# Pair products and their sums' transfers at other places, and the end of a layer shared out anew over the engines

## The chip, the cores and the metric

The kernel runs on one core of one Trainium2 chip. A core has five engines that each work through their own queue in order: TensorE (PE, matrix products into PSUM, with the weight loads shown apart as PEld), VectorE (DVE), ScalarE (ACT), GpSimd (POOL) and SyncE (SP, which here only issues transfers). POOL issues transfers too, those that add to what already lies in SBUF. The metric is the device time of one execution in microseconds; lower is better.

## The reference, cut to what matters

Two layers, each on 256 frames of 1024 channels. A layer normalises x, projects it with one wide matrix, splits the result among three token mixers and their gates, and adds the merged result back:

```python
h = _rms(x, norm_g[l])
proj = h @ w_in[l]
(gq, gk, gv, ga, gz, bq, bk, bv, iq, ik, iw, bz,
 cq, ck, cv, cz, gate) = jnp.split(proj, SPLIT_AT, axis=-1)
y_a = _gla(gq, gk, gv, ga, ...) * jax.nn.silu(gz)
y_b = _dsa(bq, bk, bv, iq, ik, iw, ...) * jax.nn.silu(bz)
y_c = _diff(cq, ck, cv, ...) * jax.nn.silu(cz)
g = jax.nn.sigmoid(gate.reshape(B, T, N_BRANCH, D_MODEL))
merged = (g[:, :, 0] * (y_a @ w_br[l, 0]) + g[:, :, 1] * (y_b @ w_br[l, 1])
          + g[:, :, 2] * (y_c @ w_br[l, 2]))
x = x + merged @ w_out[l]
```

`_gla` is a gated linear attention over chunks of 64 frames, `_dsa` scores all keys with a small indexer (iq, ik, iw), keeps the best 64 for each query and attends over those, `_diff` is the difference of two softmax attentions. Each `gate` block is a 256 x 1024 by 1024 x 512 product.

## The kernel before, in words

**Weights in two parts.** A product at full float32 accuracy is made of three products of rounded parts. A *unit* is a piece of a weight matrix of 128 x 1024 values. `Stream.split` makes of it `whi` (L230, on ACT, a copy rounded to fp32r) and `wlo` (L236, on DVE, the difference); `mm3` then issues three matmuls for each piece of a product. There are five pairs of `whi` and `wlo` buffers (`BUFS["wt"]`) and four buffers for raw units (`BUFS["raw"]`), which SP loads (L200).

**The order of the work.** `ORDER` (L36) names the pieces of a layer; `plan()` makes of it `PLAN`, a list of 104 units per layer, and `USE`, which says which places of that list a piece uses. An ordinary piece such as `bq`, `gv` or `gate0` has four units of twelve matmuls of 512 columns; `iq` and `bz` are made transposed, and hold their four units for the whole of the piece; `p..` (branch products) and `out..` have two units each.

**Pairs.** The gate blocks 2 and 3 (pair A) and 5 and 1 (pair B) are made together with Strassen's seven products instead of eight: `A1` to `A7`, `B1` to `B7`. Each of these has two units of six matmuls. Four of the seven need sums of weight blocks (`SUMS`): product 5 uses the sum called t1, product 6 t2, product 4 t4, product 7 t3. A sum is built in an SBUF tile by transfers: SP loads a first block (`begin_sum`, L217), POOL then adds a second block with an accumulating transfer (`add`, L206). t2 is t1's tile with one more block added, and t4 is t2's with one more, so those additions are issued from `split` right after t1's, or t2's, own split, and have to land before the next product of that pair is split. t1 and t3 get their first addition in `begin_sum`. `SUMS_AHEAD, SUMS_ADD = 12, 2` (L72): the load stands in the code at the split 12 places before the sum's own, the addition two splits later. The sums' tiles come from a pool of eight (`w4`), shared with key and probability tiles.

**The mixers as tasks.** The attention work is written as generators which `Flow.pump` advances; the pump is called after each group of matmuls that belongs to one of a unit's two halves (twelve matmuls' unit: two pumps). `Y` (L96) says how many pumps a task waits at each step: `dsa0` between the end of `iq` and the start of the indexer, `att0` between a selection of keys and the attention over them.

**Who sets the order on the engines.** The program is built under a planner (`tile.TileContext(nc, schedule_with_timeline_sim=True)`) that places each instruction in its engine's queue by the order of the code and by when its own timing model expects the operands. `order(a, b)` and `hold` put one instruction behind another in a queue without a wait. On the chip each queue is then worked through in that order.

**The end of a layer** (L1121 to L1144). The output product goes in four accumulators, `(n, t)` for column half and row half; row half t = 0 is finished first for both n, then t = 1. After each one DVE adds it to x (L1138) and ACT squares and sums that half (`sumsq`, L316). After n = 1, `norm_in(l + 1, t)` adds the two sums (`norm_scale`, DVE L320), raises to the power -1/2 on POOL (L321), scales the two halves of x (`norm_half`, DVE L327), transposes them on PE (L121) and writes the two parts of h, `hTh` on ACT (L336) and `hTl` on DVE (L337). The last layer writes x out instead.

Of the kernel before, what the change touches and what calls it, by code (L numbers as in the profile page):

```python
# [8 lines left out]
F32 = mybir.dt.float32  # L9
# [23 lines left out]

PAIRS = {"A": ("gate2", "gate3"), "B": ("gate5", "gate1")}

ORDER = ["bq", "cq", "ck", "gate4", "cz", "bk", "cv", "gq", "iq", "bv", "B1", "B5", "gv", "B2", "B6", "gz", "B4", "A1",  # L36
         "B3", "bz", "B7", "A5", "gate0", "A2", "p20", "A6", "p00", "A4", "p21", "A3", "A7", "p10", "p01", "p11",
         "out00", "out10", "out01", "out11"]
NAMES = [n for c in ORDER if c[0] not in PAIRS for n in (c,)] + [n for c in PAIRS.values() for n in c]


# [27 lines left out]

plan()  # L70
NPLAN = len(PLAN)
SUMS_AHEAD, SUMS_ADD = 12, 2  # L72

POOL_LO = [USE[c][i] for c, i in []]

# [13 lines left out]
MERGE_WAIT = 0  # L93
WARM = 14
AHEAD1 = (0, 2)
Y = dict(sm0=0, qk0=1, qk=3, dsa0=8, dec0=7, diff0=0, gla0=0, att0=3, top=1, blog=12, bpT=11, by=14, clog=4, cpT=2, cy=2, za=17, q2=5, st=27, go=9, sums=0)  # L96
BUFS = dict(w2=8, kp=28, w4=8, ev=2, raw=4, wt=5, ahead=21)


# [1 line left out]
def trunk(ctx: ExitStack, tc: tile.TileContext, x0, x1, units, wsmall, pack, ptmp, wa2b, out):  # L101
# [43 lines left out]
    def w4(shape, dt=F32, n="w4"):  # L145
        return sp.tile(shape, dt, tag="w4", bufs=BUFS["w4"], name=nm(n))
# [31 lines left out]
    class Stream:  # L178
# [6 lines left out]
        def hold(self, j, evac):  # L185

            if j in self.splits:
                for a, b in zip(self.splits[j], evac):
                    tc.add_manual_dep(a.ins, b.ins.name, NOSYNC, reason="order")
            else:  # L190
                self.after[j] = evac

# [12 lines left out]
            u = l * NUNIT + (UNIT[two] + 2 if what in ("t2", "t3") else UNIT[one] + (2 if what == "t4" else 0))  # L205
            G.dma_start(self.sums[l, "t3" if what == "t3" else "t1", pair, i], units[u + i], accum_op=OP.add)  # L206

        def begin_sum(self, j):
            for j, adds in ((j, False), (j - SUMS_ADD, True)):
                if j >= L * NPLAN or PLAN[j % NPLAN][0] not in ("t1", "t3"):  # L210
                    continue
                l, (what, pair, i) = j // NPLAN, PLAN[j % NPLAN]
                if adds:
                    self.add(l, what, pair, i)
                else:
                    t = self.sums[l, what, pair, i] = w4([P, 1024], F32, "sum")
                    order(nc.sync.dma_start(t, units[l * NUNIT + UNIT[PAIRS[pair][1]] + i]), self.loaded)  # L217

        def tiles(self):
            hi = wp.tile([P, 1024], F32R, tag="whi", bufs=BUFS["wt"], name=nm("whi"))  # L220
# [3 lines left out]

        def split(self):
            j = len(self.made)
            self.begin_sum(j + SUMS_AHEAD)
            raw, (hi, lo) = self.raws[j], self.tiles()
            what, *arg = PLAN[j % NPLAN]
            a = A.activation(hi, raw, AF.Copy)  # L230
            if j % NPLAN in POOL_LO:
                self.splits[j] = (a,)
                for h in HV:
                    G.tensor_sub(lo[:, h], raw[:, h], hi[:, h].bitcast(F32))
            else:
                self.splits[j] = (a, V.tensor_sub(lo, raw, hi.bitcast(F32)))  # L236
            if what in ("t1", "t2"):
                self.add(j // NPLAN, "t2" if what == "t1" else "t4", *arg)
            if j in self.after:
                self.hold(j, self.after[j])  # L240
# [79 lines left out]
        a = V.scalar_tensor_tensor(v, ss[t][:, 0:1], EPS, ss[t][:, 1:2], op0=OP.add, op1=OP.add)  # L320
        return r, a, G.tensor_tensor(r, v, half[:, :1], op=OP.pow)  # L321

    def norm_half(t, hf, r):

        ps = [at([P, 2, P], "hps") for _ in range(2)]
        h = w2([P, 512], F32, "h")
        a = V.tensor_scalar_mul(h, xs[t][:, HV[hf]], r)  # L327
        for j in range(4):
            TE.transpose(ps[j % 2][:, j // 2], h[:, j * P:(j + 1) * P], ident)
        return ps, a  # L330
# [7 lines left out]
                                       op0=OP.mult, op1=OP.subtract))  # L338

    def norm_in(l, t):  # L340
        r, _, _ = norm_scale(t)
        ps = [norm_half(t, hf, r)[0] for hf in range(2)]
        for k in range(KD8):
            e = evac(l, t, k, ps)
        if t == 0:
            ws.hold(l * NPLAN + HOLD, e)

    def project(jobs):

# [188 lines left out]
    for l in range(L):  # L538
# [584 lines left out]
        for h, n, t in ((0, 0, 0), (0, 0, 1), (0, 1, 0), (0, 1, 1), (1, 0, 0), (1, 1, 0), (1, 0, 1), (1, 1, 1)):  # L1123
            cols = [(po[n, t], slice(0, CH))]
            if (l, n, t) == (L - 1, 1, 1):
                cols = [(po[n, t][:, :256], slice(0, 256)), (po_end, slice(256, CH))]
            for ps, c in cols:
                for k in range(4):
                    wh, wl = ws.need(use(l, f"out{n}{h}")[k // 2])
                    hi, lo = mT[h, t]  # L1130
                    mm3(ps, hi[:, k], lo[:, k], wh[:, k % 2, c], wl[:, k % 2, c],
                        h == 0 and k == 0, h == 1 and k == 3)
                    if k % 2:
                        flow.pump()
                if h == 0:
                    continue
                xc = xs[t][:, n * CH + c.start:n * CH + c.stop]
                V.tensor_add(xc, ps, xc)  # L1138
                if l + 1 == L:
                    nc.sync.dma_start(out[t * P:(t + 1) * P, n * CH + c.start:n * CH + c.stop], xc)  # L1140
                else:
                    sumsq(t, n)
                    if n == 1:
                        norm_in(l + 1, t)  # L1144


def _lay_out(inputs):
# [74 lines left out]
```

## Time and profile before

| what | value |
|---|---|
| median of 3 runs | 607.3 us (606.71 to 607.91) |
| the profiled execution | 605.64 us, of which its span, first to last instruction, 603.9 us |
| granted TensorE clock | 1.000 |
| PE busy | 586.6 us (97%) |
| PEld busy | 494.6 us (82%) |
| DVE busy | 495.6 us (82%) |
| ACT busy | 378.8 us (63%) |
| POOL busy | 96.3 us (16%) |
| transfers | 121.82 MB, 202 GB/s on the mean |

Engine times are busy time and overlap each other. A row of a timeline has the start, the duration, the engine, the source line, the operation, the tile written and those read, and in brackets how long the engine had been idle and what ended that. In the list of waits a row names who waited for whom, the total in us, how many times, and the longest. The chain is the sequence of work that ended last, each piece with its start and its length. The matmuls' ends are modelled, so idle time of PE is best read from the starts.

### The profile page before, as it was taken

To read this page: it belongs to the slowest core of one execution; us is meant where nothing else is said; L and a number is where in the kernel's file an instruction comes from. 1 tells how busy PE (TensorE), PEld (TensorE's weight loads), DVE (VectorE), ACT (ScalarE), POOL (GpSimd) and SP (SyncE) were. 2 spreads that over 40 slices of the span, in tenths; PEclk is the share of its full clock that TensorE was granted. 3 is DMA by queue.
4 is the path that set the end of the run, shared out by engine and by line. 5 is a ranking of instruction groups with operands and counts; after the bars stand their busy time and mean duration, and the time that the engine had idled before them with its cause. 6 is when DMAs were issued, how large, how long until landed. Compare 5 with 4: busy or idle time off the path is not lost.

```text
span 603.9 us, 8831 instructions
## 1 busy us (share of the span) xinstructions
PE 586.6 (97%) x3118; PEld 494.6 (82%) x3118; DVE 495.6 (82%) x813; ACT 378.8 (63%) x651; POOL 96.3 (16%) x127
## 2 busy tenths in 40 slices
PE   7999999999998999999999999999999989899997
PEld 4888888998887987788878888889888878787886
DVE  6868969888979988699587796797889899759982
ACT  5759767786747465564466765876775658646540
POOL 6034212011111052000011240300102202210000
PEclk9999999999999999999999999999999999999999
DMA  8654678347897389556545445862599962994731
GB/s 334 229 185 140 216 256 234 132 139 199 277 267 221 118 246 303 173 186 236 174 140 199 151 155 196 269 217 71 175 262 277 279 226 43 341 247 138 237 114 69
DMA packets 34027, 121.82 MB, mean 202 GB/s; under 512 B 3776, under 2 KB 4160, under 8 KB 33984
## 3 DMA queue, kind: packets, MB, share of 16 engines
q1 hardware_dynamic: 29376, 104.49, 49.0%
q0 software_dynamic: 4608, 16.78, 14.5%
q8 instruction: 24, 0.39, 0.2%
q14 instruction: 19, 0.16, 0.1%
HBM read 120.21 MB, written 1.05 MB: 201 GB/s over the span
## 4 chain that ended last, share of the span: by engine, by line
PE 61%; DMA 15%; DVE 12%; issue 6%; ACT 3%; POOL 1%; SPq 0%; ACTq 0%; POOLq 0%; DVEq 0%
DMA sum<-in_units 12%; PE p L118 7%; PE out L118 6%; DVE wlo L236 5%; PE gate L118 5%; PE iq L118 4%; PE gq L118 4%; PE cq L118 4%; PE ck L118 4%; PE cz L118 4%; PE bk L118 4%; PE cv L118 4%; PE bz L118 4%; PE bq L118 3%; DMA raw<-in_units 3%
## 5 line engine op out<-in xcount | busy, mean ns | idle before, releaser
L236 DVE TENSOR_TENSOR wlo<-raw,whi 128x1024 fp32r<-128x1024 f32 x172 | 209.6, 1229 | 38.1 <-ACT whi L230 37.1
L230 ACT ACTIVATE whi<-raw 128x1024 fp32r<-128x1024 f32 x172 | 180.5, 1061 | 90.0 <-DMA raw<-in_units 28.9
L230 ACT ACTIVATE whi<-sum 128x1024 fp32r<-128x1024 f32 x32 | 33.5, 1060 | 42.5 <-DMA sum<-in_units 30.1
L236 DVE TENSOR_TENSOR wlo<-sum,whi 128x1024 fp32r<-128x1024 f32 x32 | 38.5, 1217 | 20.2 <-ACT whi L230 20.1
L290 POOL TENSOR_SCALAR v<-ss 128x4 f32<-128x4 f32 (+1 forms) x24 | 11.4, 475 | 195.6 <-DVE ss L390 94.9
L206 POOL DMA_DIRECT2D sum<-in_units x32 | 28.3, 903 | 85.8 <-DVE wlo L236 25.5
L291 POOL TENSOR_TENSOR r<-v,half 128x4 f32<-128x4 f32 (+1 forms) x24 | 33.6, 1401 | 1.8
L118 PE MATMUL p<-wlo,yTh 128*128 128x512 f32 x64 | 25.2, 395 | 1.5 <-DVE wlo L236 1.5
L118 PE MATMUL out<-wlo,mTh 128*128 128x512 f32 (+1 forms) x72 | 26.2, 368 | 0.0
L118 PE MATMUL p<-whi,yTh 128*128 128x512 f32 x64 | 25.3, 395 | 0.9 <-DVE gate L960 0.9
L118 PE MATMUL q<-wlo,sh 128*128 128x512 f32 x64 | 25.4, 397 | 0.7 <-DVE wlo L236 0.7
L118 PE MATMUL out<-whi,mTh 128*128 128x512 f32 (+1 forms) x72 | 26.0, 366 | 0.0
L118 PE MATMUL out<-whi,mTl 128*128 128x512 f32 (+1 forms) x72 | 25.7, 368 | 0.0
L118 PE MATMUL q<-whi,sl 128*128 128x512 f32 x64 | 25.1, 392 | 0.0
L118 PE MATMUL gate<-whi,hTl 128*128 128x512 f32 x64 | 25.0, 393 | 0.0
L118 PE MATMUL q<-whi,sh 128*128 128x512 f32 x64 | 25.0, 395 | 0.0
L118 PE MATMUL gate<-wlo,hTh 128*128 128x512 f32 x64 | 24.9, 390 | 0.0
L118 PE MATMUL gate<-whi,hTh 128*128 128x512 f32 x64 | 24.7, 395 | 0.0
L118 PE MATMUL p<-whi,yTl 128*128 128x512 f32 x64 | 24.6, 390 | 0.0
L118 PE MATMUL q<-whi,hTh 128*128 128x512 f32 x48 | 19.6, 408 | 1.5 <-ACT gate L1041 1.5
L118 PE MATMUL q<-wlo,hTh 128*128 128x512 f32 x48 | 18.8, 392 | 0.0
L118 PE MATMUL q<-whi,hTl 128*128 128x512 f32 x48 | 18.7, 390 | 0.0
(351 smaller groups left out, 1751.5 us busy)
## 6 DMA issues: line engine op xcount, KB each, us to landing
raw<-in_units SPq DMA_DIRECT2D x176, 512.0 KB, 4.3
sum<-in_units POOLq DMA_DIRECT2D x32, 512.0 KB, 9.4
sum<-in_units SPq DMA_DIRECT2D x16, 512.0 KB, 6.5
wsr<-in_wsmall SPq DMA_DIRECT2D x2, 416.0 KB, 6.2
xe<-in_x SPq DMA_DIRECT2D x1, 584.0 KB, 3.6
x<-in_x SPq DMA_DIRECT2D x1, 512.0 KB, 8.0
out<-xe SPq DMA_DIRECT2D x2, 256.0 KB, 2.0
pt<-in_ptmp SPq DMA_DIRECT2D x1, 384.0 KB, 9.5
```

Source lines behind the costliest of these rows:

```text
L118: return self.put(nc.tensor.matmul(*a, **k))
L206: G.dma_start(self.sums[l, "t3" if what == "t3" else "t1", pair, i], units[u + i], accum_op=OP.add)
L230: a = A.activation(hi, raw, AF.Copy)
L236: self.splits[j] = (a, V.tensor_sub(lo, raw, hi.bitcast(F32)))
L290: G.tensor_scalar(v, ss, 1.0 / dim, EPS, op0=OP.mult, op1=OP.add)
L291: G.tensor_tensor(r, v, half[:, :n], op=OP.pow)
```

## The change

Four edits. (1) `ORDER`: B1 moves from behind bv to right behind iq; gv and bv change places; A5 moves from behind B7 to right behind A1; gate0 comes before B7; A6 comes before p20 instead of behind it. (2) `SUMS_ADD` becomes 4, so that the first addition of t1 and t3 stands four splits behind its load in the code instead of two; `begin_sums` treats t1 and t3 each with its own distance (both 12). (3) `Y`: `dsa0` 8 to 6, `att0` 3 to 6; `st` is read nowhere. (4) The end of layer 0: the sum of squares of (t, n) = (0, 1) goes from ACT to DVE (`sumsq_v`, L310); the scaling of x for t = 0 goes from DVE to ACT; the `wlo` of the next layer's second unit is put behind `norm_scale`'s DVE instruction for t = 0; and ACT's sum of squares for (1, 1) is put behind the last ACT instruction of `norm_in` for t = 0. `hold` learns to skip a missing part.

```diff
-ORDER = ["bq", "cq", "ck", "gate4", "cz", "bk", "cv", "gq", "iq", "bv", "B1", "B5", "gv", "B2", "B6", "gz", "B4", "A1",
-         "B3", "bz", "B7", "A5", "gate0", "A2", "p20", "A6", "p00", "A4", "p21", "A3", "A7", "p10", "p01", "p11",
-         "out00", "out10", "out01", "out11"]
+ORDER = ["bq", "cq", "ck", "gate4", "cz", "bk", "cv", "gq", "iq", "B1", "gv", "B5", "bv", "B2", "B6", "gz", "B4",
+         "A1", "A5", "B3", "bz", "gate0", "B7", "A2", "A6", "p20", "p00", "A4", "p21", "A3", "A7", "p10", "p01",
+         "p11", "out00", "out10", "out01", "out11"]
-SUMS_AHEAD, SUMS_ADD = 12, 2
+SUMS_AHEAD, SUMS_ADD = {"t1": 12, "t3": 12}, 4
-Y = dict(sm0=0, qk0=1, qk=3, dsa0=8, dec0=7, diff0=0, gla0=0, att0=3, top=1, blog=12, bpT=11, by=14, clog=4, cpT=2, cy=2, za=17, q2=5, st=27, go=9, sums=0)
+Y = dict(sm0=0, qk0=1, qk=3, dsa0=6, dec0=7, diff0=0, gla0=0, att0=6, top=1,
+         blog=12, bpT=11, by=14, clog=4, cpT=2, cy=2, za=17, q2=5, st=30, go=9, sums=0)
                 for a, b in zip(self.splits[j], evac):
-                    tc.add_manual_dep(a.ins, b.ins.name, NOSYNC, reason="order")
+                    if b is not None:
+                        tc.add_manual_dep(a.ins, b.ins.name, NOSYNC, reason="order")
-        def begin_sum(self, j):
-            for j, adds in ((j, False), (j - SUMS_ADD, True)):
-                if j >= L * NPLAN or PLAN[j % NPLAN][0] not in ("t1", "t3"):
-                    continue
...
+        def begin_sums(self, j):
+
+            for what, ahead in SUMS_AHEAD.items():
+                for n, adds in ((j + ahead, False), (j + ahead - SUMS_ADD, True)):
+                    if n >= L * NPLAN or PLAN[n % NPLAN][0] != what:
+                        continue
+                    l, (_, pair, i) = n // NPLAN, PLAN[n % NPLAN]
+                    if adds:
+                        self.add(l, what, pair, i)
+                    else:
+                        t = self.sums[l, what, pair, i] = w4([P, 1024], F32, "sum")
+                        order(nc.sync.dma_start(t, units[l * NUNIT + UNIT[PAIRS[pair][1]] + i]), self.loaded)
-            self.begin_sum(j + SUMS_AHEAD)
+            self.begin_sums(j)
-    def norm_half(t, hf, r):
+    def norm_half(t, hf, r, on_act=False):
...
-        a = V.tensor_scalar_mul(h, xs[t][:, HV[hf]], r)
+        x = xs[t][:, HV[hf]]
+        a = A.activation(h, x, AF.Copy, scale=r) if on_act else V.tensor_scalar_mul(h, x, r)
     def norm_in(l, t):
-        r, _, _ = norm_scale(t)
-        ps = [norm_half(t, hf, r)[0] for hf in range(2)]
+        r, v, _ = norm_scale(t)
+        if t == 0:
+            ws.hold(l * NPLAN + 1, (None, v))
+        ps = [norm_half(t, hf, r, t in (0,))[0] for hf in range(2)]
...
+        return e
...
-                    sumsq(t, n)
+                    square = (sumsq_v if (t, n) == (0, 1) else sumsq)(t, n)
+                    if (t, n) == (1, 1):
+                        order(square, behind[0])
                     if n == 1:
-                        norm_in(l + 1, t)
+                        behind = norm_in(l + 1, t)
```

More of the change, by code (lines that the diff above doesn't have):

```diff
@@ L71 @@
 NPLAN = len(PLAN)
-SUMS_AHEAD, SUMS_ADD = 12, 2
-POOL_LO = [USE[c][i] for c, i in []]
+SUMS_AHEAD, SUMS_ADD = {"t1": 12, "t3": 12}, 4
+POOL_LO = []
 def columns(*widths):
@@ L206, in add @@
             G.dma_start(self.sums[l, "t3" if what == "t3" else "t1", pair, i], units[u + i], accum_op=OP.add)
-        def begin_sum(self, j):
-            for j, adds in ((j, False), (j - SUMS_ADD, True)):
-                if j >= L * NPLAN or PLAN[j % NPLAN][0] not in ("t1", "t3"):
-                    continue
[L212 to L217, printed above, removed]
+        def begin_sums(self, j):
[9 more added lines that the diff above has]
+                        order(nc.sync.dma_start(t, units[l * NUNIT + UNIT[PAIRS[pair][1]] + i]), self.loaded)
         def tiles(self):
```

## The prediction

> **What bounds the kernel now.** I read the page first, then the list of PE's waits, then the timelines around each wait.
>
> ```profile
> PE 586.6 (97%) x3118; PEld 494.6 (82%) x3118; DVE 495.6 (82%) x813; ACT 378.8 (63%) x651; POOL 96.3 (16%) x127
> ...
> raw<-in_units SPq DMA_DIRECT2D x176, 512.0 KB, 4.3
> ```
>
> PE is busy for 97% of the span, and the change takes away no matmul, so only PE's waits can go. They are few:
>
> ```profile
> PE blog L118 <- DVE sd L896: 2.6, 2, 1.3
> PE hps L121 <- DVE h L327: 2.0, 2, 1.2
> PE pT L121 <- DVE bp L722: 1.7, 2, 1.0
> PE q L118 <- ACT gate L1041: 1.5, 2, 0.8
> PE p L118 <- DVE wlo L236: 1.5, 2, 1.0
> ...
> PE p L118 <- DVE gate L960: 0.9, 2, 0.5
> PE q L118 <- DVE wlo L236: 0.7, 2, 0.5
> ```
>
> All but `hps` come once per layer; of `hps` 1.2 us is the layer's end, the rest the kernel's start, which the change leaves alone. Together 2.6 + 1.2 + 1.7 + 1.5 + 1.5 + 0.9 + 0.7 = 10.1 us: the most that this change can bring, short of smaller gaps that the list leaves out. All are waits for DVE or ACT, and the longest waits of ACT itself are for the sums:
>
> ```profile
> ACT whi L230 <- DMA sum<-in_units: 30.1, 8, 5.7
> ```
>
> **(a) The layer's end.**
>
> ```profile
> 303.91 0.39 PE L118 MATMUL out<-wlo,mTh 128*128 128x512 f32 x1
> 304.14 0.39 PE L118 MATMUL out<-whi,mTl 128*128 128x512 f32 x1
> 305.76 1.06 PE L121 MATMUL hps<-xe,h 128*128 128x128 f32 x8 [1.24 <-DVE h L327]
> ...
> 300.26 0.69 DVE L1138 TENSOR_TENSOR xe<-out,xe 128x512 f32<-128x512 f32 x1 [2.71 <-PE out L118]
> 301.63 1.23 DVE L236 TENSOR_TENSOR wlo<-raw,whi 128x1024 fp32r<-128x1024 f32 x1 [0.68 <-ACT whi L230]
> ...
> 303.37 0.15 DVE L320 SCALAR_TENSOR_TENSOR v<-ss 128x1 f32<-128x1 f32 x1
> ...
> 305.13 0.88 DVE L327 TENSOR_SCALAR h<-xe,r 128x512 f32<-128x512 f32 x2 [0.47 <-POOL r L321]
> ...
> 300.53 1.06 ACT L230 ACTIVATE whi<-raw 128x1024 fp32r<-128x1024 f32 x1 [2.23 <-issue]
> 301.50 0.61 ACT L316 ACTIVATE junk<-xe 128x512 bf16<-128x512 f32 x1
> ...
> 303.67 1.42 POOL L321 TENSOR_TENSOR r<-v,half 128x1 f32<-128x1 f32 x1 [67.06 <-DVE v L320]
> ...
> 4.31 0.69 DVE L310 CUSTOM_DVE_ANT_0 junk<-xe 128x512 f32<-128x512 f32 x1 [3.19 <-DMA xe<-in_x]
> ```
>
> Matmuls of 512 columns start 0.23 us apart, so the last `out` product is through at 304.4, and the transposes start at 305.76. What keeps them: x is ready at 300.95, but the square stands behind a `whi` on ACT, and `v` behind a `wlo` on DVE, until 303.37. With the change the square runs on DVE right behind the addition (0.69, and 0.1 to read the sum: until 301.7), `v` is out at 301.9 since the `wlo` now stands behind it, POOL's power takes 0.2 + 1.42 (303.5), ACT's scaling of a half about the 0.61 of its square (304.1; on DVE it took 0.44). That is before 304.4: the wait of 1.24 goes, I take 1.2. Bounds: 0 if ACT puts the scaling behind two more `whi`, 1.4 with the gap between starts. The moved `wlo` is of the second unit and starts at 301.9 instead of 301.63, under the remaining `out` products; the last square of t = 1, now behind eight `hTh`, has bq's matmuls for t = 0 over it, 24 at 0.23 us.
>
> **(b) The first additions and A5.** The later place of the first additions I cost at nothing, from 0 to 0:
>
> ```profile
> 91.31 0.87 POOL L206 DMA_DIRECT2D sum<-in_units  x1 [2.35 <-DMA sum<-in_units]
> ```
>
> This is B5.1's addition. In the code it stands at the split of iq's second unit; it was issued as soon as its load had landed, during gq. The planner issues it when the operand should be there, wherever it stands. What moves the transfers is `ORDER`:
>
> ```profile
> 153.33 6.57 DMA sum<-in_units
> ...
> 160.49 2.64 POOL L206 DMA_DIRECT2D sum<-in_units  x3 [5.94 <-PE gv L118]
> 169.21 0.88 POOL L206 DMA_DIRECT2D sum<-in_units  x1 [6.08 <-PE q L118]
> ...
> 156.52 1.21 DVE L236 TENSOR_TENSOR wlo<-sum,whi 128x1024 fp32r<-128x1024 f32 x1
> ...
> 173.92 1.22 DVE L236 TENSOR_TENSOR wlo<-sum,whi 128x1024 fp32r<-128x1024 f32 x1 [3.35 <-ACT whi L230]
> ...
> 177.71 1.22 DVE L236 TENSOR_TENSOR wlo<-sum,whi 128x1024 fp32r<-128x1024 f32 x1 [0.71 <-ACT whi L230]
> ...
> 170.00:200.00 30.00, 28.03 (x161) 24.08 (x160) 25.94 (x48) 17.36 (x28) 4.29 (x7) 1.00 0.85 246
> ```
>
> B7.0's load lands at 153.33 + 6.57 = 159.90, and POOL, whose queue has that addition first, stands still for it until 160.49. B4.0's addition, free since B6.0's `wlo` ended at 157.73, goes out behind it and moves behind it. So DVE gets B4.0 at 173.92 and B4.1 at 177.71, and idles 3.35 + 0.71 = 4.06 us: exactly its whole idle time between 170 and 200 (30.00 - 25.94). DVE is the bound of that stretch, and PE waits there for 1.97 us (30.00 - 28.03), behind a late `wlo` of B3 and the late `sd`.
>
> By places in `PLAN`: B7 and A5 were 66 to 69, with loads at 54 to 57, just between B6 (50, 51) and B4 (56, 57). Now A5 is 60, 61 with loads at 48, 49, ahead of B6, and B7 is 72, 73 with loads at 60, 61, behind B4. No first addition stands between B6 and B4 any more, and DVE starts on B4 up to 4.06 us earlier. A5's two splits, which now come ahead of bz, cost DVE 2 x 1.22 = 2.4, and give PE 12 matmuls x 0.23 = 2.8 more cover. So 4.06 - 1.97 + 0.4 = 2.5 us to spare. Of blog's 2.6 and q's 0.7 (both layers) I take 2.6, between 0 and 3.3.
>
> **(c) The second half of DSA.** `pT` (1.7) and `q` behind ACT's copy of A5's result (1.5) are accidents of the place in the queue. A5 now stands far ahead of A2, so the second may go. `att0` moves `pT` by one pump against the order (two earlier, three later), but A2 is now one of six short products in a row. I take 1.0, between 3.2 and a loss of 9.0 (third rival).
>
> **(d) A6 ahead of p20.**
>
> ```profile
> 231.14 1.22 DVE L236 TENSOR_TENSOR wlo<-sum,whi 128x1024 fp32r<-128x1024 f32 x1
> ...
> 243.54 1.23 DVE L236 TENSOR_TENSOR wlo<-sum,whi 128x1024 fp32r<-128x1024 f32 x1 [3.99 <-ACT whi L230]
> 247.40 1.23 DVE L236 TENSOR_TENSOR wlo<-sum,whi 128x1024 fp32r<-128x1024 f32 x1 [2.63 <-ACT whi L230]
> ...
> 232.76 0.86 POOL L206 DMA_DIRECT2D sum<-in_units  x1 [2.76 <-DVE bpT L733]
> ...
> 235.75 10.45 DMA sum<-in_units
> ```
>
> A6.0's `wlo` ends at 232.36 and A4.0's starts 11.2 us later, after its addition. PE has between them A6.1 and p00: 6 + 24 matmuls, 6.9 us. DVE idles 6.6 us and the later `wlo` and `gate` reach PE late: 1.5 + 0.9. Now p20 and p00 lie between, 54 matmuls or 12.4 us, which covers 11.2. I take 2.0, between 0 and 2.4.
>
> **(e) B1 behind iq, and `dsa0`.**
>
> ```profile
> L118 PE MATMUL dots<-ikh,iqe x16: 220/276/283, 143.0 to 456.7; 128*128 128x128 f32 x8, 128*128 128x256 f32 x8
> ...
> 137.83 0.69 DVE L634 TENSOR_TENSOR iqo<-iq,iqo 64x512 fp32r<-64x512 f32 x1
> ```
>
> The indexer's first matmul, at 143.0, had 4.5 us after its operand `iqo` (138.52). It now comes two pumps (2.8) earlier, and B1's four pumps last 2.8 instead of 5.5, together 5.5: at 137.5. A wait of up to 1.0 per layer appears if the planner lets it, against 0; I take 0.3, so -0.6, between -2.0 and 0.
>
> **Sum:** 1.2 + 2.6 + 1.0 + 2.0 - 0.6 = 6.2 us. The profiled execution would go from 605.64 to 599.4; it lies 1.66 below the median of the runs, so I forecast 607.3 - 6.2 = **601.1 us**. With all of the waits gone it is 607.3 - 10.3 = 597.0.
>
> **The rivals.** *First, the loads of raw units pay.*
>
> ```profile
> 143.25 7.25 DMA raw<-in_units
> ...
> 151.69 1.23 DVE L236 TENSOR_TENSOR wlo<-raw,whi 128x1024 fp32r<-128x1024 f32 x1 [1.40 <-ACT whi L230]
> ```
>
> Beside B6's two additions a raw unit took 7.25 us instead of the page's 4.3, and DVE lost 1.40 for it. A5's loads and additions now fall into this same stretch; three such losses eat the 4.06 of (b). Then (b) and (c) bring nothing: 1.2 + 2.0 - 0.6 = 2.6, 604.7 us. Against it: the transfers leave a stretch that was fuller (0.85 of the DMA engines from 170 to 200). The Trainium skill, "DMA: Bandwidth & Descriptors", section "Queues, rings and completion order", says that each DMA engine takes turns between the queues that have work, packet by packet, which speaks for this case; the 7.25 agrees.
>
> *Second, the sums' edits do nothing*, because the planner again puts a first addition ahead of B4's and A4's. Only (a) is left: 606.1 us. For it: the distance in the code already had no say at 91.31. Against: A5's loads go out well before B6's `wlo`.
>
> *Third, slower: six short products in a row.* B7, A2 and A6 now follow each other, with the second half of DSA among them.
>
> ```profile
> 219.25 1.12 DVE L915 SCALAR_TENSOR_TENSOR ya<-go,f,gz 128x128 f32<-128x128 f32 x4
> ...
> 226.63 1.13 DVE L722 TENSOR_SCALAR bp<-bp,rs 128x256 f32<-128x256 f32 x4
> ```
>
> PE needs 36 x 0.23 = 8.3 us for them. DVE needs six splits (7.3), five additions of the products (0.69 each, 3.4), two `ya` (2.2), `bp` (1.1) and about four more of 0.69 (2.8): 16.8. Five weight buffers leave a lead of three short units, 4.1. If all of that work falls there, PE waits 16.8 - 8.3 - 4.1 = 4.4 per layer: 607.3 - (1.2 + 2.6 + 2.0 - 0.6) + 8.8 = 610.9 us. It decides once the other work in that run passes 5.1 us (8.3 + 4.1 - 7.3). Against it: the planner can put `ya` and `bp` before or behind.
>
> **How the numbers follow.** Forecast 0.58, first rival 0.20, second 0.10, third 0.12. About 0.2% (1.2 us) is what a measurement can tell from no change. Forecast, first rival and a quarter of the second (0.03) are faster: 0.80; the rest of the second is within: 0.08; the third is slower: 0.12. The range goes from 597.0, where no wait is left, to 608.0, which holds the first two rivals; the likeliest case alone spans 597.0 to 604.
>
> **What would show it.** (a) `hps` at the layer's end without a wait above 0.3, the square of the second half on DVE. (b) POOL's additions for B4 within 1 us of B6's `wlo`; ACT's wait for sums down from 30.1 to under 10; DVE without the two idle stretches. (d) A4's `wlo` with under 1 us of idle time before it. (c) and the third rival: PE's waits between gate0 and p20. (e) `dots` with a wait for `iqo`. I am wrong if PE's waits stay at 8 us or more, or if new ones for `wlo` appear at B7, A2 and A6.

## The result, and the profile after

The changed kernel takes **591.63 us** (median; 591.33 to 591.70), the kernel before, beside it, 607.25 us (606.71 to 607.91): a ratio of 0.9741, 95% interval 0.9724 to 0.9758. I had forecast 601.1 us with a range from 597.0. The change is faster, as forecast, but by 15.6 us instead of 6.2, and the result lies below the range, under a floor that I had called the most that the change can bring. The profiled execution took 591.33 us with a span of 589.5 us (before: 605.64 and 603.9).

The page of the changed kernel: the engines' busy time, and the transfers into sums.

```profile
PE 582.6 (99%) x3118; PEld 495.5 (84%) x3118; DVE 494.6 (84%) x813; ACT 381.0 (65%) x651; POOL 94.7 (16%) x127
...
sum<-in_units POOLq DMA_DIRECT2D x32, 512.0 KB, 7.5
```

The chain that ends last is PE itself for 96% of the span: little else is left to wait for. An addition into a sum lands 7.5 us after its issue (median). PE's idle time, span less busy, fell from 603.9 - 586.6 = 17.3 to 589.5 - 582.6 = 6.9 us, by 10.4. But its *busy* time fell too, by 4.0 us, with the same 3118 instructions. 10.4 + 4.0 is the 14.4 us of the span; the second part I had not foreseen at all.

PE's longest waits in the changed kernel (total, times, longest), and ACT's waits that answer to the "sums" row of before:

```profile
PE bq L119 <- DVE wlo L492: 1.3, 2, 0.7
...
PE hps L122 <- ACT h L332: 0.5, 1, 0.5
PE bq L119 <- ACT hTh L341: 0.2, 1, 0.2
PE hps L122 <- DVE h L332: 0.2, 1, 0.2
```

```profile
ACT whi L234 <- PE p L119: 28.4, 18, 2.8
...
ACT whi L234 <- DMA raw<-in_units: 9.7, 12, 2.1
...
ACT whi L234 <- DMA sum<-in_units: 1.4, 1, 1.4
```

The first and last of these rows of PE's list are the kernel's start. The waits of `blog`, `pT`, `q` and `p`, 8.9 us of the 10.1 that I had listed, are gone in both layers; of the layer's end 0.5 + 0.2 is left. ACT waits 1.4 us for sums instead of 30.1, and now mostly for PE to give weight buffers back.

The changed kernel's timelines of DVE and of POOL around B4 (and DVE's at A4), and then one stretch of it by windows (start and end, length, busy time and number of PE, PEld, DVE, ACT and POOL, granted clock, DMA share, GB/s):

```profile
155.93 1.21 DVE L240 TENSOR_TENSOR wlo<-sum,whi 128x1024 fp32r<-128x1024 f32 x1
158.76 1.21 DVE L240 TENSOR_TENSOR wlo<-sum,whi 128x1024 fp32r<-128x1024 f32 x1
169.50 1.23 DVE L240 TENSOR_TENSOR wlo<-sum,whi 128x1024 fp32r<-128x1024 f32 x1
173.35 1.22 DVE L240 TENSOR_TENSOR wlo<-sum,whi 128x1024 fp32r<-128x1024 f32 x1
...
233.53 2.35 DVE L240 TENSOR_TENSOR wlo<-sum,whi 128x1024 fp32r<-128x1024 f32 x2
...
157.50 0.86 POOL L208 DMA_DIRECT2D sum<-in_units  x1 [4.97 <-DVE work L676]
160.38 0.88 POOL L208 DMA_DIRECT2D sum<-in_units  x1 [2.03 <-DVE work L676]
```

```profile
170.00:200.00 30.00, 30.00 (x176) 26.44 (x175) 29.12 (x54) 20.33 (x38) 6.34 (x7) 1.00 0.94 270
```

B6's two `wlo` end at 157.14 and 159.97; B4's additions go out 0.4 us behind each of them (before: behind B7's first addition, which went out at 160.49). A5's first additions stand ahead of them in POOL's queue, but went out at 149.02 and 151.50. B4's own `wlo` start at 169.50 and 173.35 without idle time (before: 173.92 and 177.71, after 3.35 and 0.71 idle). Between 170 and 200 us DVE works for 29.12 of 30 us instead of 25.94, and PE without a pause. A4's two `wlo` (233.53) come without idle time as well (before: 3.99 and 2.63).

### The profile page after: what moved, and what is told of

It is laid out like the page before. It is cut to its first block, busy times and chain, and to the rows that moved or that the text cites. A ratio compares the mean times of both kernels' runs of the same rounds, so it can differ in the third digit from the quotient of the medians.

```text
span 589.5 us, 8843 instructions
## 1 busy us (share of the span) xinstructions
PE 582.6 (99%) x3118; PEld 495.5 (84%) x3118; DVE 494.6 (84%) x813; ACT 381.0 (65%) x651; POOL 94.7 (16%) x127
## 4 chain that ended last, share of the span: by engine, by line
PE 96%; DMA 1%; ACT 1%; DVE 1%; POOL 1%; issue 0%; SPq 0%; DVEq 0%; POOLq 0%
PE q L119 13%; PE p L119 11%; PE gate L119 7%; PE out L119 7%; PE bz L119 4%; PE iq L119 4%; PE gq L119 4%; PE ck L119 4%; PE cq L119 4%; PE gz L119 4%; PE cz L119 4%; PE gv L119 4%; PE bv L119 4%; PE bk L119 4%; PE cv L119 4%; PE bq L119 3%
## 5 line engine op out<-in xcount | busy, mean ns | idle before, releaser
L294 POOL TENSOR_SCALAR v<-ss 128x4 f32<-128x4 f32 (+1 forms) x24 | 7.6, 315 | 224.8 <-DVE ss L398 92.5
L119 PE MATMUL p<-whi,yTh 128*128 128x512 f32 x64 | 24.1, 392 | 0.0
```

The costliest lines, as they stand in the source:

```text
L119: return self.put(nc.tensor.matmul(*a, **k))
L294: G.tensor_scalar(v, ss, 1.0 / dim, EPS, op0=OP.mult, op1=OP.add)
```

## The experiments

In the runs of these experiments the kernel before had medians of 605.96 to 606.25, 1.2 us less than beside the changed kernel's first runs; the changed kernel itself repeated at 591.47. So times against the kernel before are read here from 606.0, and times against the changed kernel from 591.5. The ratios are to the kernel before. The kernels called "before + ..." are the changed kernel with its other edits taken back.

| kernel | median us | ratio, 95% interval |
|---|---|---|
| before + new ORDER alone | 594.81 | 0.9814 (0.9790 to 0.9838) |
| before + new pumps alone | 615.45 | 1.0135 (1.0083 to 1.0188) |
| before + POOL's queue alone | 596.18 | 0.9839 (0.9809 to 0.9870) |
| before + POOL's queue + new pumps | 605.95 | 0.9993 (0.9968 to 1.0018) |
| before + A5, gate0, B7 moved alone | 594.56 | 0.9791 (0.9761 to 0.9820) |
| before + A6 moved alone | 604.21 | 0.9962 (0.9943 to 0.9980) |
| changed, old ORDER | 611.87 | 1.0091 (1.0059 to 1.0123) |
| changed, t3's loads earlier | 609.99 | 1.0056 (1.0042 to 1.0070) |
| changed, old pumps | 593.98 | 0.9802 (0.9775 to 0.9829) |
| changed, att0 = 3 | 593.67 | 0.9779 (0.9755 to 0.9803) |
| changed, old layer's end | 592.25 | 0.9777 (0.9753 to 0.9801) |
| changed, SUMS_ADD = 2 | 591.56 | 0.9764 (0.9741 to 0.9787) |
| changed, A6 behind p20 again | 591.62 | 0.9752 (0.9727 to 0.9776) |
| changed, B1, gv, bv as before | 591.79 | 0.9756 (0.9732 to 0.9780) |
| changed, again | 591.47 | 0.9751 (0.9727 to 0.9775) |
| changed, layer's end, first attempt | 591.32 | 0.9748 (0.9723 to 0.9772) |
| changed, x's addition behind v | 590.81 | 0.9744 (0.9717 to 0.9771) |
| changed, both | 590.76 | 0.9742 (0.9715 to 0.9769) |

Most of the intervals are some 0.005 wide, 3 us, so two rows that lie closer are not parted by them; there I go by the medians, the ranges of the runs and the trace.

The changed kernel once more, as the measure for small differences:

> The changed kernel itself, as a measure for the three others on the same chip: 591.6, or less by the 1.2 us by which the kernel before was faster here in the earlier experiments (606.0 against 607.2).

### Each edit taken back from the changed kernel

```diff
 # (1) a_noorder: ORDER as in the kernel before
 # (2) a_noend
-        if t == 0:
-            ws.hold(l * NPLAN + 1, (None, v))
-        ps = [norm_half(t, hf, r, t in (0,))[0] for hf in range(2)]
+        ps = [norm_half(t, hf, r)[0] for hf in range(2)]
...
-                    square = (sumsq_v if (t, n) == (0, 1) else sumsq)(t, n)
-                    if (t, n) == (1, 1):
-                        order(square, behind[0])
+                    square = sumsq(t, n)
 # (3) a_noy: dsa0=8, att0=3
 # (4) a_noadd: SUMS_ADD = 2
```

> The changed kernel with the old ORDER; the other three edits stay. The prediction's prices (2.6 for the sums' transfers around B4, 2.0 for A6 ahead of p20, most of 1.0 for the second half of DSA, 0.3 lost for B1) give 591.6 + 5.3 = 597. If ORDER alone removed every wait in the middle of the layers, with the whole gaps between starts of matmuls (4.55 at B3 and blog, 3.84 at pT and q, 3.11 at the branch products, both layers, and about 2 us of small gaps), it is 591.6 + 13.5 = 605. If the pumps of the tasks removed the waits of pT and q, 591.6 + 9.7 = 601.

> The changed kernel with the layer's end as before (square of the second half and scaling of x back on their old engines, no holding of the second unit's wlo, the last square free). The prediction has 1.2 us for it: 592.8. By the starts of matmuls, where 0.62 before hps and 0.37 before bq remain of the 1.40 of before, it is 0.4: 592.0. Nothing else in the layers should differ.

> The changed kernel with dsa0 = 8 and att0 = 3 as before. If the waits of pT and q are gone because the sums come in time (the prediction's reason), nothing changes beyond the 0.6 booked against dsa0: 591.0 to 592. If att0 took them away, the 3.84 of gaps at pT and q come back: 595.4.

> The changed kernel with the first addition of t1 and t3 two splits behind its load in the code instead of four. By the prediction it costs nothing: POOL's queue keeps its order and the time is 591.6. The rival: the addition is put ahead of others in POOL's queue, which then stands still until its load has landed, and with t4's additions late again, 1 to 3 us are lost: 592.6 to 594.6.

Without the new ORDER the rest of the change is a loss: 611.87, slower than the kernel before, outside all three numbers expected. The old pumps cost 593.98 - 591.5 = 2.5 us, neither 0 nor 3.9. The old end of the layer costs 0.8 by the medians, with all else alike (592.02 to 593.42 against 591.29 to 591.73). SUMS_ADD costs nothing (591.56), as forecast. The parts don't add up, so next each was put into the kernel before by itself.

### ORDER alone, the pumps alone

```diff
 # b_order: the kernel before with the new ORDER
 # b_y: the kernel before with
-Y = dict(... dsa0=8 ... att0=3 ...)
+Y = dict(... dsa0=6 ... att0=6 ...)
```

> The kernel before with the new ORDER alone. By the prediction's prices (2.6 + 2.0 + 1.0 - 0.3) 607.2 - 5.3 = 602. If the new ORDER alone removes the whole gaps between starts in the middle of the layers (4.55 + 3.84 + 3.11 = 11.5), it is 595.7. By the change without its ORDER (611.9) the pumps of the tasks cost time under the old ORDER only; then this run lies within 2.4 us (the price of the pumps under the new ORDER) and 0.7 (the layer's end) of the changed kernel: 594.7.

> The kernel before with dsa0 = 6 and att0 = 6 alone. If the pumps are worth under the old ORDER what they were worth under the new one (2.4 us), it is 604.8; by the prediction 607.8 (0.6 lost for dsa0). If they are what made the change without its ORDER slower than the kernel before (611.9), it is 611 to 613, with a wait of ACT for the DSA's maxima, and of PE's q for whi and wlo, near 190 and 224 us.

ORDER alone gives 606.0 - 594.8 = 11.2 us: the gain of the second number, of whole gaps between starts (11.5), and the time of the third (594.7), and far from the 5.3 us of my prices. The pumps alone lose 9.4 us, more than the third number there. The same two numbers in `Y` are worth +9.4 us under the old ORDER and -2.5 under the new one.

### POOL's queue alone

The prediction's mechanism for (b) was that POOL stands still for the load of a sum that is needed later, while an addition that is needed sooner waits behind it. That can be had without moving a product:

```diff
-SUMS_AHEAD, SUMS_ADD = 12, 2
+SUMS_AHEAD, SUMS_ADD = {"t1": 12, "t3": 12}, 4
...
             a = G.dma_start(self.sums[...], units[u + i], accum_op=OP.add)
+            if what == "t4":
+                self.t4[l, pair] = a
+            return a
...
-                        self.add(l, what, pair, i)
+                        a = self.add(l, what, pair, i)
+                        if what == "t3" or pair == "A":
+                            order(a, self.t4[l, pair if what == "t3" else "B"])
```

> The kernel before, where only POOL's queue is changed: the first additions of B7 and A5 stand behind both additions for B4, and those of A7 behind both for A4 (written out as an order on the engine; SUMS_ADD is 4 so that the code allows it). All products keep their places. If a first addition that stands still for its load ahead of B4's and A4's additions is what makes their sums late, as the prediction says, the gaps of 4.55 at B3 and blog and of 3.11 at the branch products go: 607.2 - 7.7 = 599.5, and at least 604.5 at the prediction's 2.6 for the first of the two. If the places of the products around them decide, it stays at 606 to 608.

It gives 606.0 - 596.2 = 9.8 us, more than the 7.7 of the whole gaps named; by the starts of matmuls `pT` gave 1.4 too, which I had not expected of it. PE's waits that are left, POOL's additions and ACT's `whi` of B4 in this kernel:

```profile
PE q L118 <- ACT gate L1051: 1.6, 2, 0.8
...
PE hps L121 <- DVE h L336: 1.2, 1, 1.2
...
PE pT L121 <- DVE bp L732: 0.5, 1, 0.5
```

```profile
158.74 0.87 POOL L207 DMA_DIRECT2D sum<-in_units  x1 [3.54 <-DVE work L678]
...
168.88 1.06 ACT L238 ACTIVATE whi<-sum 128x1024 fp32r<-128x1024 f32 x1 [1.85 <-DVE work L678]
172.69 1.06 ACT L238 ACTIVATE whi<-sum 128x1024 fp32r<-128x1024 f32 x1 [1.40 <-DMA sum<-in_units]
```

B4.0's addition goes out at 158.74 instead of behind B7's at 160.49, and B4's two sums are there 3.9 us earlier than before (168.88 and 172.69 against 172.82 and 176.62 on ACT), about the 3.8 us that lie between the two. The waits for `sd`, for `wlo` of q and p and for `gate` are gone, those for A4 as well as for B4; `q` behind ACT's `gate`, part of `pT` and the layer's end stay.

At A4 it isn't POOL's standing still that costs. POOL's additions of A7 in the kernel before:

```profile
226.66 0.94 POOL L206 DMA_DIRECT2D sum<-in_units  x1 [4.17 <-DMA sum<-in_units]
229.15 0.86 POOL L206 DMA_DIRECT2D sum<-in_units  x1 [1.56 <-DMA sum<-in_units]
```

POOL does wait for their loads, but A4.0's addition still goes out at 232.76, 0.4 us after A6.0's `wlo` has ended, so it was not held back. It is slow in landing, with A7's two still moving ahead of it: ACT gets A4.0 at 242.45, 9.7 us after the issue. With A7's behind it, in this kernel, that is 5.7 us (229.63 to 235.30).

The reverse, in the changed kernel: t3's loads stand earlier in the code, so that POOL's queue again has first additions for B7 ahead of B4's.

```diff
-SUMS_AHEAD, SUMS_ADD = {"t1": 12, "t3": 12}, 4
+SUMS_AHEAD, SUMS_ADD = {"t1": 12, "t3": 24}, 4
```

> The changed kernel in which only t3's sums begin earlier: B7's and A7's loads stand 24 splits ahead in the code instead of 12, so that B7's first additions come into POOL's queue ahead of B4's and one of A7's ahead of each of A4's, as in the kernel before. All products keep their new places. If POOL's queue decides, the gaps at B3 and blog come back, 4.55 us, and at the branch products, 3.11: 596 to 599; at the prediction's prices (2.6 and 2.0) 594.2 to 596.2. If the places of the products decide, it stays at 591.6 to 592.5.

609.99: the whole gain and more is gone, though every product stands at its new place. B7's first additions are indeed ahead of B4's; those of A7, though, come among A6's additions and not, as I had written, ahead of A4's. Nor is it a load that B4's additions stand behind here. In every kernel of this case at most three of POOL's additions are in flight, and where a fourth is due it goes out 0.31 us after the first of the three has landed. So here: three additions of A5 and B7 land at 158.06, 161.89 and 166.78, and the next go out at 158.37, 162.20 and 167.09. The last two of these are B4's, though B6.0's `wlo` ended at 156.76. And the amount is not that of the late B4 alone. The timelines of ACT and PE, then a window, then the transfers issued from 186 to 206 us (KB each, median us to landing):

```profile
174.50 1.06 ACT L234 ACTIVATE whi<-sum 128x1024 fp32r<-128x1024 f32 x1 [3.98 <-DMA sum<-in_units]
...
202.73 1.06 ACT L234 ACTIVATE whi<-raw 128x1024 fp32r<-128x1024 f32 x1 [6.32 <-DMA raw<-in_units]
...
203.84 0.58 PE L119 MATMUL bz<-hTh,whi 128*128 128x256 f32 x1 [3.90 <-ACT whi L234]
...
502.05 0.58 PE L119 MATMUL bz<-hTh,whi 128*128 128x256 f32 x1 [4.82 <-ACT whi L234]
```

```profile
204.00:210.00 6.00, 6.00 (x29) 6.00 (x30) 4.48 (x7) 3.35 (x9) 0.00 (x0) 0.50 0.79 287
```

```profile
raw<-in_units SPq DMA_DIRECT2D x5, 512.0 KB, 9.1
sum<-in_units POOLq DMA_DIRECT2D x4, 512.0 KB, 9.1
```

In the changed kernel the same view has:

```profile
raw<-in_units SPq DMA_DIRECT2D x7, 512.0 KB, 4.2
```

B4's sum is late again (3.98 us of idle ACT). A second loss, which no theory had here, is larger: four additions, A6's and A7's, now share the DMA engines with the raw units of bz; a raw unit takes 9.1 us instead of 4.2, ACT idles 6.32 us for one, and PE stands still at bz for 3.90 us, and for 4.82 in the second layer. The third loss is in the window: after that pause the granted clock is 0.50 for six microseconds. By the starts of PE's instructions, the gaps around B3 and blog come to 3.1 us for both layers, those at bz to 9.6, and the half rate to about 5.7: together 18.4 of the 18.5 us that were lost. So the place of t3's transfers is enough to lose the gain, but only 3 of the 18 us are the late B4; the rest comes through the raw units.

### Single moves of ORDER

```diff
 # b_a5, in the kernel before
-         "B3", "bz", "B7", "A5", "gate0", "A2", ...
+         "A5", "B3", "bz", "gate0", "B7", "A2", ...
 # b_a6, in the kernel before
-         ... "p20", "A6", "p00", ...
+         ... "A6", "p20", "p00", ...
 # a_noa6, in the changed kernel: "p20", "A6", "p00"
 # a_noiq, in the changed kernel: "iq", "bv", "B1", "B5", "gv"
```

> The kernel before with A5 behind A1 and gate0 ahead of B7, and nothing else. A5's loads then stand ahead of B6's splits and B7's behind, so POOL has no first addition between B6 and B4: the gaps at B3 and blog go, 607.2 - 4.55 = 602.7; with those of pT and q too (3.84) 598.8; at the prediction's 2.6 it is 604.6. If the planner still puts a first addition there, 607.

> The kernel before with A6 put ahead of p20 and nothing else. The prediction takes 2.0 us of 2.4 for it: 605.2; by the whole gaps between starts 3.1: 604.1. If the products' places make a new wait (A2 and A6 behind each other, with their splits, while the second half of DSA is made), the gain is eaten: 607 to 609.

> The changed kernel with A6 behind p20 again, all else as changed. If the prediction's 2.0 for A6 ahead of p20 holds (the move alone, in the kernel before, gave 1.9), it is 593.6. If moving A5 and B7 has already taken A4's lateness away, as the new ORDER's 594.8 beside that move's 594.6 suggests, the move is worth nothing here: 591.6, with the same small gaps.

> The changed kernel with bv, B1, B5, gv in the old order behind iq. The prediction booked -0.3 us for B1 and -0.3 for dsa0, so taking the move back would gain: 591.0 to 591.3. If the indexer's operand is early enough, as the changed kernel's trace shows no wait there, nothing happens: 591.6. If iq's place moves B6's and B4's additions (A5's loads come 8 units sooner or later against them), 592 to 594.

The move of A5, gate0 and B7 alone is worth 606.0 - 594.6 = 11.4 us, all that ORDER is worth and more than any of the four numbers expected. A6's move is worth 1.8 us in the kernel before (604.21), near the prediction's 2.0, but not by its working. `p`'s waits for `wlo` and `gate` fall from 2.4 to 0.4 us, as forecast. But A4's sums reach ACT only at 242.19 and 245.94, and the `whi` that follow them keep PE waiting at `q` instead, until 249.01 in the first layer:

```profile
PE q L118 <- ACT whi L233: 4.0, 2, 2.1
```

What is gained comes from `pT` and `q` behind ACT's `gate`, whose 3.2 us are gone too. In the changed kernel A6's move is worth nothing (591.62). A4's sums are still late there with A6 behind p20: ACT waits 10.6 us for them in the two layers, and DVE idles 1.91 and 2.18 in the first. But no wait of PE comes of it. B1's move is worth nothing that can be told (591.79).

### The pumps

```diff
 # b_yq: POOL's queue as in b_q, and dsa0=6, att0=6
 # a_att3: the changed kernel with att0=3, dsa0=6
```

> The kernel before with the pumps of the change (dsa0 = 6, att0 = 6), which alone made it 615, and with POOL's queue in the order that alone made it 596.2 (first additions of B7, A5 and A7 behind those for B4 and A4). If the pumps lose their time only because they put more first additions ahead of B4's, they are now worth what they were worth under the new ORDER (2.4 us gained): 593.8. If the pumps themselves delay the mixers, it is 596.2 + 8 = 604 or more.

> The changed kernel with att0 = 3 as before and dsa0 = 6. The two pumps together were worth 2.4 us. If att0 earned it, 593.4 to 594.0; if dsa0 did, against the prediction's 0.6 lost, 591.6.

`att0` earns 593.67 - 591.5 = 2.2 of the 2.5 us of both pumps under the new ORDER; the 0.3 left for `dsa0` can't be told from nothing (593.15 to 594.10 and 592.99 to 594.75). My theory that they lose time under the old one only through POOL's queue has fallen: with that queue mended it is 605.95, not 593.8. PE's timeline there, a window, and ACT's waits:

```profile
223.26 0.65 PE L119 MATMUL q<-whi,hTh 128*128 128x512 f32 x1 [2.30 <-ACT whi L239]
223.70 0.63 PE L119 MATMUL gate<-wlo,hTh 128*128 128x512 f32 x1
...
226.69 0.48 PE L119 MATMUL gate<-whi,hTh 128*128 128x512 f32 x1
227.00 0.39 PE L119 MATMUL gate<-wlo,hTh 128*128 128x512 f32 x1
```

```profile
223.00:227.00 4.00, 3.74 (x9) 2.95 (x10) 3.76 (x7) 2.80 (x4) 0.00 (x0) 0.57 1.00 409
```

```profile
ACT whi L239 <- DMA raw<-in_units: 35.1, 21, 5.3
...
ACT whi L239 <- DMA sum<-in_units: 2.7, 2, 1.6
```

The sums are in time (2.7 us), but ACT waits 35.1 us for raw units (28.9 before), and PE 2.30 us at 223.26 for a raw unit of the product behind gate0, A2, in a stretch where the DMA engines are full (share 1.00). Why the pumps make those raw units late under the old ORDER, and not under the new one, stays open.

### The end of the layer

```diff
 # a_end2, in norm_half for t = 0, first half; and the squares of t = 1
+            a = A.activation(h[:, :P], x[:, :P], AF.Copy, scale=r)
+            A.activation(h[:, P:], x[:, P:], AF.Copy, scale=r)
...
-                    if (t, n) == (1, 1):
+                    if t == 1:
                         order(square, behind[0])
 # a_end3v, alone; a_end3 has all three
-                V.tensor_add(xc, ps, xc)
+                xa = V.tensor_add(xc, ps, xc)
+                if (t, n) == (1, 0) and l + 1 < L:
+                    order(xa, behind[2])      # behind[2]: v of t = 0
```

> The changed kernel with two more changes at the layer's end: ACT scales the first 128 columns of x by themselves ahead of the other 384, so that the first transpose can start sooner, and both squares of t = 1, not only the second, stand behind ACT's last hTh for t = 0. Of the gaps of 0.62 before hps and 0.37 before bq, 0.3 to 0.7 us should go: 590.9 to 591.3. The rival: the squares of t = 1 are then late and the second half's transposes wait: 591.6 to 593.

> The changed kernel, in which DVE's addition of x for (t, n) = (1, 0) stands behind v of t = 0. If that addition (0.69 us between the square and v) is what the prediction's 1.2 missed, v comes at 294.5 instead of 295.1, POOL's power ends 0.6 earlier, and the wait of 0.46 before hps goes: the gap falls from 0.62 to under 0.2 and the time to 591.0. If another thing holds ACT's scaling (a whi ahead of it until 295.6), the gap stays at 0.5 or more and the time at 591.5.

> The same with the two edits of the earlier attempt at the layer's end (ACT scales the first 128 columns ahead of the rest; both squares of t = 1 behind ACT's last hTh). All of the 0.62 and 0.37 us would go but 0.1 to 0.2: 590.6 to 590.8 against the changed kernel's 591.5. If the squares of t = 1 are then late, 591.5 or more.

The changed kernel's timelines of PE, DVE, ACT and POOL at that place:

```profile
296.81 0.39 PE L119 MATMUL out<-whi,mTl 128*128 128x512 f32 x1
297.65 1.27 PE L122 MATMUL hps<-xe,h 128*128 128x128 f32 x8 [0.46 <-ACT h L332]
299.13 0.50 PE L119 MATMUL bq<-whi,hTh 128*128 128x512 f32 x1 [0.21 <-ACT hTh L341]
...
294.27 0.08 DVE L314 DVE_READ_ACCUMULATOR2_ANT ss<- 128x1 f32 x1
294.52 0.69 DVE L1146 TENSOR_TENSOR x<-out,x 128x512 f32<-128x512 f32 x1 [0.16 <-PE out L119]
295.12 0.15 DVE L324 SCALAR_TENSOR_TENSOR v<-ss 128x1 f32<-128x1 f32 x1
...
296.88 1.34 ACT L332 ACTIVATE h<-xe,r 128x512 f32<-128x512 f32 x2 [1.25 <-POOL r L325]
...
295.43 1.42 POOL L325 TENSOR_TENSOR r<-v,half 128x1 f32<-128x1 f32 x1 [70.00 <-DVE v L324]
```

And with the addition behind `v`:

```profile
296.99 0.39 PE L119 MATMUL out<-whi,mTl 128*128 128x512 f32 x1
297.23 1.27 PE L122 MATMUL hps<-xe,h 128*128 128x128 f32 x8
...
294.64 0.16 DVE L324 SCALAR_TENSOR_TENSOR v<-ss 128x1 f32<-128x1 f32 x1
```

The transposes now start 0.24 us behind the last `out` product's start, that is, at once. 590.81 against 591.47 is 0.66 us, about the gap of 0.62 that was left; the ratios' intervals overlap, but the ranges of the two don't (590.71 to 591.12 and 591.29 to 591.73). The other two edits alone give 591.32 (the gap before `bq` goes, but the one before `hps` is then 0.30 + 0.40), and on top of this one 590.76: nothing that can be told. The version with the addition behind `v` beats both kernels, by 0.1% over the changed one.

## Why the prediction was right and wrong

**The sign and the mechanism of (b)** were right. That POOL's queue holds B4's addition behind a first addition that stands still for its load was read off the trace of before, and mending that queue alone gives 9.8 us, A4's part among them.

**The step that failed first** is "the change takes away no matmul, so only PE's waits can go", with the 10.1 us "the most that this change can bring". The list's idle time is not what a wait costs. PE's timeline of the kernel before at the branch products:

```profile
252.77 0.42 PE L118 MATMUL p<-whi,yTh 128*128 128x512 f32 x1
254.20 0.50 PE L118 MATMUL p<-wlo,yTh 128*128 128x512 f32 x1 [1.01 <-DVE wlo L236]
254.53 0.40 PE L118 MATMUL p<-whi,yTl 128*128 128x512 f32 x1
```

Start to start it is 1.43 us where 0.23 is the rule, so 1.20 are lost, while the list has 1.01: the modelled end of a matmul lies 0.16 to 0.19 us behind the start of the next one in a running stream, and that tail counts as busy. The matmul after the wait then takes 0.33 to the next start, 0.10 more than the rule. So this wait costs 1.30, not 1.01. My list had 13 waits; at some 0.27 us each that is 3.5 us, most of the 4.0 by which PE's busy time fell. The floor should have stood at about 607.3 - 13.6 = 593.7. The 591.6 lies lower still, by the rest of that busy time and by the last two items of the next paragraph.

**The second step** is the share that I took of the list. I booked 6.2 net, of which 0.6 were a loss; 10.1 - 0.7 = 9.4 went. With the 4.0 of busy time and 1.0 of idle time elsewhere (0.6 of it `hps` at the kernel's start, 0.8 before and 0.2 after, which is not the change's: the changed kernel, run again, has none, and with `att0` = 3 it has 0.5) this makes the 14.4 us of the span: 6.2 + 3.2 + 4.0 + 1.0. The other 1.2 us of the 15.6 are not in the two profiles: the profiled execution of before lies 1.6 us below its median, that of the changed kernel 0.3. Against the 606.0 of the later runs the change is worth 14.5.

Term by term:

- **(a)**, 1.2: measured 0.7 to 0.8, with 0.46 left before `hps` where I had asked for 0.3 at most. The mis-sized step is "`v` is out" 0.2 us behind the square: DVE's queue has x's addition for (1, 0) between the two, and `v` comes at 295.12, 0.8 behind the square's read-out. Taken away, the rest of the 1.2 comes in. The same addition stood between the `wlo` and `v` in the kernel before, where the prediction put `v`'s lateness down to the `wlo` alone:

```profile
302.77 0.68 DVE L1138 TENSOR_TENSOR x<-out,x 128x512 f32<-128x512 f32 x1
```

- **(b)**, 2.6, and the first additions' later place, 0: the latter holds in the changed kernel (591.56); under the old ORDER it was not tried alone. The former was much too small: A5, gate0 and B7 alone bring 11.4, of which the gaps at B3 and `blog` are 4.55 by the starts. The rest are waits that I had under (c) and (d). A4's sums were late through POOL's queue too, though there because A7's additions were moving ahead of them, not because POOL stood still. With A5 moved alone, A6's additions also go out early (183.96 and 187.99 instead of 211.81 and 213.78), so that the stretch up to A4 holds four additions instead of six; how much each of the two brings no run parts. Of `pT` and `q`, the queue alone takes 1.2 of `pT`'s 1.7 and nothing of `q` behind ACT's `gate`.
- **(c)**, 1.0 between 3.2 and -9.0: all of the 3.2 went. Both waits go where A5 moved, as I had half expected of `q`, but also where A6 alone moved, so my word for them, accidents of the place in the queue, isn't contradicted and no single cause is shown. `att0`, which I counted as one pump against the order, earns 2.2 us, but not at these two waits: with the old pumps under the new ORDER neither comes back. With `att0` = 3 in the changed kernel one wait of 1.2 us appears (`q` for ACT's `yTh`), and with both old pumps two others (`blog` 0.7, `p` 0.4); why the pumps remove these is not shown.
- **(d)**, 2.0: the number came out in the kernel before (1.8), by luck. The step that failed is the cover: the lateness of A4's sums moved on to `q`, where it costs 4.0 us against the 2.0 that `p`'s waits lost, and the gain is the 3.2 of `pT` and `q`. In the change the term is zero. My working, 11.2 us to be covered by 12.4 us of matmuls, took the addition's 10.45 us as given; much of it was the lateness. In the changed kernel PE does not wait at A4 with A6 behind p20 either.
- **(e)**, -0.6: nothing that can be told. I had the indexer start at 137.5 against an operand that stayed at 138.52. The operand moved too: in the changed kernel's timeline and list of groups `iqo` is done at 130.89, and the first `dots` starts at 141.8.

```profile
130.20 0.69 DVE L642 TENSOR_TENSOR iqo<-iq,iqo 64x512 fp32r<-64x512 f32 x1
```

```profile
L119 PE MATMUL dots<-ikh,iqe x16: 273/278/306, 141.8 to 446.1; 128*128 128x128 f32 x8, 128*128 128x256 f32 x8
```


**The rivals.** The first, the loads of raw units, did not come in the changed kernel (ACT's waits for them fell from 28.9 to 9.7), but it is what ruined two of the experiments, at a higher price than I had given it. There the Trainium skill's rule, "DMA: Bandwidth & Descriptors", section "Queues, rings and completion order", that a DMA engine takes turns between the queues that have work, agrees: five raw units beside four additions took 9.1 us each instead of 4.2. The second, the planner putting a first addition ahead again, did no harm: those of A5 and A7 do stand ahead of B4's and A4's, but went out 6 us and more before them. The third, six short products in a row, did not come: no wait stands at B7, A2 or A6.

**Why the parts don't add up.** Undone singly: ORDER 20.4, pumps 2.5, layer's end 0.8, SUMS_ADD 0. Alone: ORDER 11.2, pumps -9.4. I had added terms as if each could be had without the others.

## What to carry to other kernels

A queue that stands still for a transfer delays whatever stands behind it: look first at what an in-order queue has in front of the late transfer, and at what that one waits for, since a reordering of the queue alone can be most of the gain. A transfer that was issued in time can be late as well, where others issued before it are still moving. A wait of PE in a list of idle time costs more than the list says where the ends of matmuls are modelled, so measure from start to start before calling a sum a floor. And an edit's price is that in its company: the same two numbers were worth 9.4 us one way and 2.5 the other.

## What was not expected of the hardware

After a long pause PE ran at half rate for some microseconds. In the kernel before with POOL's queue and the new pumps, matmuls of 512 columns start 0.43 us apart from 223.26 on, after a pause of 2.30 us, and 0.23 apart again from 227.00; the granted clock of that window is 0.57. After the 3.90 us at bz it lasts until 210.2, 6.4 us. The half of that time that is lost comes on top of the pause: 1.9 us on 2.30, and 3.2 on 3.90, so these two cost some 1.8 times their length. The Trainium skill, "TensorE: Matmul & The Clock Gate", section "Part 1: The HAM clock gate (the "warmup" mystery)", has the halving and gives the idle time that brings it as one window of about 3.4 us; here a pause of 2.30 was enough, while one of 2.46 us in the changed kernel with the old ORDER passed at full rate:

```profile
224.59 0.50 PE L119 MATMUL q<-whi,hTh 128*128 128x512 f32 x1 [2.46 <-ACT whi L234]
```

```profile
224.50:228.50 4.00, 3.91 (x17) 3.21 (x18) 3.93 (x7) 2.65 (x4) 0.45 (x1) 1.00 1.03 421
```

So at this length the length alone doesn't decide; what does, no run here shows. The pauses of the kernel before, 1.3 us and less, brought none in its profile (granted clock 1.000). Its times, and more so those of the kernels with the long pauses, scatter more (604.1 to 609.3 us, and 609.9 to 616.5 with the pumps alone) than the changed kernel's (591.3 to 591.7). A lowered clock in some executions is part of that: of the kernel before's 62 executions in the experiments, the 21 with a mean granted clock of 0.997 or less have a median of 607.4 us, the 41 others 605.9. Three thousandths of 606 us are 1.8 us, so the sizes fit; that it is the half rate behind a longer pause is likely, but none of these was profiled.
